# Holding both token halves of a linear open, and dividing the probabilities in place

## The chip, the cores and the metric

The kernel runs on one core of one Trainium2 chip. The metric is the device time of one execution in microseconds (us), lower is better. The kernel before took 2855.56 us, the median of 3 runs (2854.57 to 2858.59).

## What is computed

One inference step of a trunk of two layers with 1024 channels, for 128 context tokens and 512 latent tokens, 640 tokens in all. Cut to what matters here, a layer is:

```
h   = rms_norm(x) * (1 + scale1) + shift1
cb, cc, cx, aq, ak, av, dn_q, dn_k, dn_v, dn_z, dn_beta, dn_a, gate_logits = split(h @ w_in)
ya  = (cb * conv3(cc * cx)) @ w_pa                                  # short gated convolution
yb  = softmax(q @ keys.T * 128**-0.5) @ vals @ w_pb                 # 8 heads, 2 key-value heads
yc  = gated_deltanet_both_directions(dn_q, dn_k, dn_v, ...) @ w_pc  # 4 heads, chunked scan
mix = (ga * ya + gb * yb + gc * yc) @ w_o
x   = x + gate1 * rms_norm(mix)
ffn = (silu(h2 @ w_gate) * (h2 @ w_up)) @ w_down                    # h2: norm of x, 2816 wide
x   = x + gate2 * rms_norm(ffn)
```

Context tokens attend to themselves (128 keys); latent tokens attend to 128 cached keys and their own 512, so a row of probabilities has 640 entries. All data are fp32.

## The kernel before

Activations lie channel by token: a tile has 128 channels on the partitions and 640 tokens in the free dimension, and each is kept as a pair of fp32r tiles, a rounded high part and the rest (`hh`). A **linear** computes 128 output channels for all 640 tokens. Its weights come in blocks of up to four k-tiles (128x128 each). For a block, the SP queue starts a DMA into one of three raw tiles (`wraw`, tag `wr`, NWR = 3); ScalarE casts it to the high part `whi`, VectorE subtracts to get `wlo` (`split`, lines 93 to 95); `whi` and `wlo` have three buffers each (NW = 3). Each k-tile takes three matmuls (`mm3`, lines 362 to 365): high by high, high by low, low by high. The 640 tokens are done as two halves of 320 columns, each in a PSUM bank of its own from a ring of three (`lbank`, NL = 3). `linear` (lines 394 to 398) loads all blocks and runs `lin_half` for half 0 over all k-tiles, then for half 1. After a half, `ev` moves the sums out of the bank, on ScalarE or VectorE according to the linear: `sg` and `fs` (gates and feed-forward), `ccs`, `padc`, `padf`, `cz` (convolution and DeltaNet inputs). Most linears have eight k-tiles, in two blocks; `w_pa` and `w_pc` have four, in one; the first part of the down projection has 14, in four. `group` and the last six linears of `lin_res` keep their weight blocks and call `lin_half` themselves.

**Attention** (`attn_head`, lines 695 to 780). Per head there are three stages: query tiles 1 and 2, query tiles 3 and 4 (256 latent queries at a time), and the prompt. `a_sample` computes scores with queries on the partitions; `soft` (lines 702 to 724) takes the maximum, lets ScalarE write exp to `p` (128 queries by 640 keys) with its row sums, and inverts the sum on VectorE. It then builds `dg`, the identity times the inverse, from a ring of two tiles (NDG). `b_sample` multiplies `p` by `dg` on TensorE, key tile by key tile, into the tile `ptT` (lines 759 to 768): this transposes `p` and divides it by its sum in one step. The result is split and multiplied by the values (lines 775 to 777), into `po`. The prompt does the same at line 738 (`psp`) on 128 keys. The main loop (lines 1278 to 1293) keeps up to two stages (NPD = 2) between the softmax and the transposes.

**Order.** The program is written as generators: a main chain (DeltaNet, then attention) whose steps yield assumed costs, and a fill chain of linears that `run` and `weave` place between them. The tile framework then plans the order of the instructions on each engine before the run, by priority and its own model of when things are ready. On the chip each engine takes its queue in that order and waits by semaphores. The DeltaNet stretch of a layer has a long chain on VectorE (the elimination of lines 977 to 982, into `Tt`) and loads rows broadcast over partitions on the SP queue (`rowb`, line 899).

Of the kernel before, what the change touches and what calls it, by code (L numbers as in the profile page):

```python
# [14 lines left out]
P = 128  # L15
NT = 640
HF = NT // 2
# [13 lines left out]
NL, NB = 3, 5  # L31
NH_, NC_, NF_, NT_ = 16, 24, 16, 4
NWR, NW = 3, 3
NXO, NRR, NVW, NDG = 3, 3, 2, 2

KEEP = ("C", "C", "C", "C", "E", None)
LEAD = ("C", "C", "C", "C", "E")
# [15 lines left out]
def tile_trunk(ctx: ExitStack, tc: tile.TileContext, I: dict, O: list, layers=DEPTH):  # L53
    nc = tc.nc
    V, A, T, G, SY = nc.vector, nc.scalar, nc.tensor, nc.gpsimd, nc.sync
# [5 lines left out]
    def slot(name, shape=(P, NT), dt=F32, tag="F"):  # L61
        n = {"H": NH_, "C": NC_, "F": NF_}[tag]
        return sb.tile(list(shape), dt, tag=tag, name=name, bufs=n)

    def cslot(name, shape=(P, NT), dt=F32):
        return slot(name, shape, dt, "C")
# [4 lines left out]
    def lbank():  # L71
        return pp.tile([P, 512], F32, tag="l", name="l", bufs=NL)

    def bank(name):
        return pp.tile([P, 512], F32, tag="c", name=name, bufs=NB)

    def small(name, shape, bufs, dt=F32):
        return sb.tile(list(shape), dt, tag=name, name=name, bufs=bufs)

    def hv(t, h):  # L80
        return t[:, h * HF:(h + 1) * HF]
# [11 lines left out]
    def split(hi, lo, src):  # L93
        A.copy(hi, src)  # L94
        V.tensor_sub(lo, src, hi.bitcast(F32))  # L95
# [7 lines left out]
    ident = small("ident", (P, P), 1)  # L103
# [115 lines left out]
    pt = bank("c2")  # L219
# [137 lines left out]
    def wblock(src, nk, keep=None):  # L357
        raw = sb.tile([P, nk, P], F32, tag="wr", name="wraw", bufs=NWR)
        SY.dma_start(out=raw, in_=src.rearrange("(k p) f -> p k f", p=P))
        return wsplit(raw, [P, nk, P], keep)  # L360

    def mm3(out, wh, wl, ah, al, first, last):
        T.matmul(out, lhsT=wh, rhs=ah, start=first, stop=False)  # L363
        T.matmul(out, lhsT=wh, rhs=al, start=False, stop=False)  # L364
        T.matmul(out, lhsT=wl, rhs=ah, start=False, stop=last)  # L365

    def wblocks(src, nk, keep=None):
        out = []
        k = 0
        if keep == "E":  # L370
            hi, lo = [sb.tile([P, 8, P], F32R, tag="E", name="wk", bufs=3) for _ in range(2)]
            for k in range(0, nk, 4):
                raw = sb.tile([P, 4, P], F32, tag="wr", name="wraw", bufs=NWR)
                SY.dma_start(out=raw, in_=src[k * P:(k + 4) * P].rearrange("(k p) f -> p k f", p=P))
                split(hi[:, k:k + 4], lo[:, k:k + 4], raw)
            return [(hi, lo, nk)]
        while k < nk:
            n = min(4, nk - k)
            hi, lo = wblock(src[k * P:(k + n) * P], n, keep)
            out.append((hi, lo, n))  # L380
            k += n
        return out

    def lin_half(blocks, acts, h, ev):
        pb = lbank()[:, :HF]
        i = 0
        for hi, lo, nk in blocks:
            for j in range(nk):
                ah, al = acts[i]
                mm3(pb, hi[:, j, :], lo[:, j, :], hv(ah, h), hv(al, h), i == 0, i == len(acts) - 1)  # L390
                i += 1
        ev(h, pb)

    def linear(src, acts, ev):

        bl = wblocks(src, len(acts))
        for h in range(2):
            lin_half(bl, acts, h, ev)

    def group(items, side=None):  # L400

# [47 lines left out]
    def lin_res(srcw, acts, ys, gs, keeps, part, after, end=False):  # L449
# [20 lines left out]
        for m in range(n0):  # L470
            linear(w(m), acts, ev(m))
# [33 lines left out]
    def gate(l, b, m, tag="F"):  # L505

        c0 = COL["gate"] + b * D + m * P
        sg = slot("sg", tag=tag)
        linear(I["w_in"][l, :, c0:c0 + P], cur["h"], sig_ev(sg))
        return sg  # L510
# [184 lines left out]
    def attn_head(l, h, kv, qs):  # L695
        KT, KP, Vh, Vl = kv
        g = h // 4
        qh, ql, rq = qs[h]
        of = slot(f"o{h}")
        hd = slice(g * P, (g + 1) * P)  # L700

        def soft(c, parts):

            n = sum(x.shape[-1] for x in parts)
            nb, s = small("nb", (P, 2), 4), small("ssum", (P, 2), 4)
            rc = rq[:, 2 * c:2 * c + 1]
            for i, x in enumerate(parts):
                V.tensor_reduce(out=nb[:, i:i + 1], in_=x, axis=AX.X, op=ALU.max, negate=True)
            if len(parts) == 2:
                V.scalar_tensor_tensor(out=nb[:, 0:1], in0=nb[:, 0:1], scalar=nb[:, 1:2], in1=rc, op0=ALU.min, op1=ALU.mult)  # L710
            else:
                V.tensor_mul(nb[:, 0:1], nb[:, 0:1], rc)
            p = cslot("p", (P, n))
            o_ = 0
            for i, x in enumerate(parts):
                w = x.shape[-1]
                A.activation(p[:, o_:o_ + w], x, AF.Exp, scale=rc, bias=nb[:, 0:1], accum_out=s[:, i:i + 1])
                o_ += w
            if len(parts) == 2:
                V.tensor_add(s[:, 0:1], s[:, 0:1], s[:, 1:2])  # L720
            V.reciprocal(s[:, 0:1], s[:, 0:1])
            dg = small("dg", (P, P), NDG)
            V.tensor_scalar_mul(dg, ident, s[:, 0:1])
            return p, dg


        kh, kl = KT[g]
        kp = KP[g]

        def a_prompt():  # L730
            psc = bank("psc")[:, :P]
            mm3(psc, qh[:, 0:P], ql[:, 0:P], kp[:, 0, :], kp[:, 1, :], True, True)
            return [soft(0, [psc])]

        def b_prompt(sm_):
            p, dg = sm_[0]
            psc = bank("psp")
            T.matmul(psc[:, 0:P], lhsT=p, rhs=dg, start=True, stop=True)
            pth = cslot("pth", (P, 2, P), F32R)
            split(pth[:, 0, :], pth[:, 1, :], psc[:, 0:P])  # L740
            mm3(psc[:, P:2 * P], Vh[0][:, 0, hd], Vl[0][:, 0, hd], pth[:, 0, :], pth[:, 1, :], True, True)
            A.copy(of[:, 0:P], psc[:, P:2 * P])

        def a_sample(pr2):
            out = []
            for c in (1 + 2 * pr2, 2 + 2 * pr2):
                cs = slice(c * P, (c + 1) * P)
                parts = []
                for h_ in range(2):
                    b = bank("sco")[:, :HF]  # L750
                    mm3(b, qh[:, cs], ql[:, cs], hv(kh, h_), hv(kl, h_), True, True)
                    parts.append(b)
                out.append(soft(c, parts))
            return out

        def b_sample(pr2, sm_):
            tt = []
            for j in range(3):
                pt = bank("ptT").rearrange("p (i n) -> p i n", i=2)
                m = 2 if j < 2 else 1  # L760
                for i in range(m):
                    kt = 2 * j + i
                    for q in range(2):
                        T.matmul(pt[:, i, q * P:(q + 1) * P], lhsT=sm_[q][0][:, kt * P:(kt + 1) * P], rhs=sm_[q][1],  # L764
                                 start=True, stop=True)
                th, tl = cslot("pTh", (P, 2, 256), F32R), cslot("pTl", (P, 2, 256), F32R)
                split(th[:, :m], tl[:, :m], pt[:, :m])
                tt.append((th, tl))
            po = bank("po")[:, 0:256]
            for kt in range(5):  # L770
                vi = 5 if kt == 0 else kt
                vh, vl = Vh[vi // 2][:, vi % 2, hd], Vl[vi // 2][:, vi % 2, hd]
                th, tl = tt[kt // 2]
                th, tl = th[:, kt % 2, :], tl[:, kt % 2, :]
                T.matmul(po, lhsT=vh, rhs=th, start=(kt == 0), stop=False)  # L775
                T.matmul(po, lhsT=vl, rhs=th, start=False, stop=False)
                T.matmul(po, lhsT=vh, rhs=tl, start=False, stop=(kt == 4))  # L777
            A.copy(of[:, P + pr2 * 256:P + (pr2 + 1) * 256], po)

        return [(a_sample, b_sample, 0), (a_sample, b_sample, 1), (a_prompt, b_prompt, None)], of  # L780


# [466 lines left out]
    for p in range(2):  # L1249
        mod_first(p)  # L1250
        if p == 0:
            first = lead(0)
            for i in range(1, NLD):
                w, a, ev, k = first[3][i]
# [6 lines left out]
    for l in range(layers):  # L1261
# [61 lines left out]
        acts, acts2 = [], []  # L1323
# [77 lines left out]
```

## Time and profile before

| | us |
|---|---|
| median of 3 runs | 2855.56 |
| lowest, highest | 2854.57, 2858.59 |
| the profiled execution | 2858.44 |
| its span, first instruction to last | 2856.7 |

| engine | busy us | share of the span | instructions |
|---|---|---|---|
| PE (TensorE matmul) | 2767.4 | 97% | 20042 |
| PEld (its weight loads, beside PE) | 2637.4 | 92% | 20042 |
| DVE (VectorE) | 1539.8 | 54% | 3275 |
| ACT (ScalarE) | 1252.4 | 44% | 2863 |
| POOL (GpSimd) | 112.2 | 4% | 235 |

One execution is profiled, so durations are of that execution, and its own time is set beside them. PE's busy time is the union of records that overlap one another: a matmul's record spans its way through the array, and the next starts before it ends. The distance from start to start says what one costs in a stream. "Idle before, releaser" is the time an engine stood still before an instruction and what ended that. The granted clock (PEclk) is 1.00 at 2.4 GHz and 0.50 at 1.2 GHz; its mean is 0.984. The layers' stages lie, for layer 0 and layer 1, at about 80 to 560 and 1500 to 2000 us (DeltaNet, convolution and gates), 588 to 791 and 2013 to 2210 us (attention), and 950 to 1450 and 2360 to 2800 us (feed-forward).

### The profile page before, as it was taken

The page shows a single profiled execution, that of the slowest core. Times are in us where ns is not written, and L with a number is a line of the kernel's source. Part 1 is how long each engine was busy: PE and PEld are TensorE (multiplying, and loading weights), DVE is VectorE, ACT ScalarE, POOL GpSimd, SP SyncE. Part 2 cuts the span into 40 slices and gives each one's busy share as a digit, 9 for nine tenths or more (in the row PEclk, how much of TensorE's full clock was granted, in tenths as well). Part 3 has the DMA queues.
Part 4 walks back from the last instruction along what each step waited for, and adds up shares of the span by engine and source line. Part 5 has one row for each costly group of instructions (what it writes and reads, how often), then busy time and mean ns, then how long its engine had stood idle before and what let it go on. Part 6 is the DMA issues. An engine that isn't in the chain of part 4 may idle for free.

```text
span 2856.7 us, 50458 instructions
## 1 busy us (share of the span) xinstructions
PE 2767.4 (97%) x20042; PEld 2637.4 (92%) x20042; DVE 1539.8 (54%) x3275; ACT 1252.4 (44%) x2863; POOL 112.2 (4%) x235
## 2 busy tenths in 40 slices
PE   7999999999999999999989899999999999999998
PEld 4898998999999899999978889989999999999997
DVE  4576566466643744224465765764677446442344
ACT  4433543465534533223455335435655354332334
POOL 1000000000000200000020000000000020000002
PEclk9999999999999999999999999999999999999999
DMA  7441354333364444444443423443232433222232
GB/s 245 75 83 43 83 102 114 81 64 91 116 183 135 145 131 141 130 154 144 133 114 72 74 44 83 102 99 84 62 93 90 115 105 97 75 73 77 73 111 75
DMA packets 401562, 293.52 MB, mean 103 GB/s; under 512 B 19318, under 2 KB 365228, under 8 KB 401324
## 3 DMA queue, kind: packets, MB, share of 16 engines
q1 hardware_dynamic: 401324, 290.28, 38.9%
q8 instruction: 157, 2.57, 0.4%
q14 instruction: 81, 0.66, 0.1%
HBM read 257.10 MB, written 33.11 MB: 102 GB/s over the span
## 4 chain that ended last, share of the span: by engine, by line
PE 80%; DVE 8%; DMA 7%; ACT 3%; issue 2%; POOL 0%; SPq 0%; DVEq 0%; ACTq 0%; POOLq 0%
PE l L363 21%; PE l L365 21%; PE l L364 21%; DMA rowb<-gd 3%; PE ptT L764 3%; DMA wraw<-in_w_in_dram 2%; PE pm L324 1%; DVE wlo L95 1%; DVE Tt L982 1%; DVE tmpE L980 1%; PE sco L363 1%; PE po L775 1%; PE po L777 1%; PE scan L1061 1%; PE sco L365 1%
## 5 line engine op out<-in xcount | busy, mean ns | idle before, releaser
L95 DVE TENSOR_TENSOR wlo<-wraw,whi 128x512 fp32r<-128x512 f32 (+1 forms) x540 | 370.2, 687 | 587.9 <-ACT whi L94 575.2
L94 ACT CAST whi<-wraw 128x512 fp32r<-128x512 f32 (+1 forms) x540 | 330.4, 613 | 733.6 <-PE l L364 654.6
L363 PE MATMUL l<-hh,whi 128*128 128x320 f32 x1856 | 593.4, 320 | 16.1 <-ACT whi L94 14.2
L365 PE MATMUL l<-hh,wlo 128*128 128x320 f32 x1856 | 588.1, 317 | 10.9 <-DVE wlo L95 10.9
L364 PE MATMUL l<-hl,whi 128*128 128x320 f32 x1856 | 584.7, 315 | 0.0
L363 PE MATMUL l<-h2h,whi 128*128 128x320 f32 x1248 | 387.7, 311 | 0.0
L364 PE MATMUL l<-h2l,whi 128*128 128x320 f32 x1248 | 385.8, 309 | 0.0
L365 PE MATMUL l<-h2h,wlo 128*128 128x320 f32 x1248 | 385.7, 309 | 0.0
L363 PEld LDWEIGHTS l<-hh,whi 128*128 128x128 f32 x1856 | 355.2, 191 | 21.6 <-ACT whi L94 16.4
L365 PEld LDWEIGHTS l<-hh,wlo 128*128 128x128 f32 x1856 | 355.1, 191 | 16.3 <-DVE wlo L95 15.0
L364 PEld LDWEIGHTS l<-hl,whi 128*128 128x128 f32 x1856 | 355.0, 191 | 1.9
L363 PEld LDWEIGHTS l<-h2h,whi 128*128 128x128 f32 x1248 | 234.7, 188 | 7.0 <-ACT fs L417 3.1
L364 PEld LDWEIGHTS l<-h2l,whi 128*128 128x128 f32 x1248 | 234.7, 188 | 0.0
L365 PEld LDWEIGHTS l<-h2h,wlo 128*128 128x128 f32 x1248 | 234.7, 188 | 0.0
L363 PE MATMUL l<-ah,whi 128*128 128x320 f32 x544 | 170.3, 314 | 0.0
L365 PE MATMUL l<-ah,wlo 128*128 128x320 f32 x544 | 168.0, 309 | 0.0
L364 PE MATMUL l<-al,whi 128*128 128x320 f32 x544 | 167.9, 309 | 0.0
L152 POOL TENSOR_TENSOR acc<-acc,sqt 128x320 f32<-128x320 f32 x88 | 86.3, 980 | 2020.8 <-ACT sqt L148 2018.3
L364 PE MATMUL l<-rsl,whi 128*128 128x320 f32 x384 | 119.0, 311 | 0.2
L365 PE MATMUL l<-rsh,wlo 128*128 128x320 f32 x384 | 119.0, 310 | 0.0
L363 PE MATMUL l<-rsh,whi 128*128 128x320 f32 x384 | 118.3, 312 | 0.0
L363 PEld LDWEIGHTS l<-ah,whi 128*128 128x128 f32 x544 | 102.3, 188 | 5.0 <-ACT whi L94 2.8
(428 smaller groups left out, 5477.7 us busy)
## 6 DMA issues: line engine op xcount, KB each, us to landing
wraw<-in_w_in_dram SPq DMA_DIRECT2D x256, 256.0 KB, 4.6
wm<-in_w_mod_dram SPq DMA_DIRECT2D x80, 512.0 KB, 5.7
wraw<-in_w_gate_dram SPq DMA_DIRECT2D x88, 256.0 KB, 3.0
wraw<-in_w_up_dram SPq DMA_DIRECT2D x88, 256.0 KB, 3.1
wraw<-in_w_down_dram SPq DMA_DIRECT2D x80, 256.0 KB, 3.1
rowb<-gd SPq DMA_DIRECT2D x32, 320.0 KB, 9.4
mixo<-mixd SPq DMA_DIRECT2D x32, 320.0 KB, 6.6
wm<-in_w_mod_dram SPq DMA_DIRECT2D x32, 256.0 KB, 3.9
```

The source lines that it names most:

```text
L94: A.copy(hi, src)
L95: V.tensor_sub(lo, src, hi.bitcast(F32))
L152: (V if n == 2 else G).tensor_add(accs[0], accs[0], t)
L324: T.matmul(pm[32 * u:32 * u + 2, 0:256], lhsT=sc[:, k, :], rhs=w[:, u * 256:(u + 1) * 256], start=(n == 0), stop=(n == KD - 1))
L363: T.matmul(out, lhsT=wh, rhs=ah, start=first, stop=False)
L364: T.matmul(out, lhsT=wh, rhs=al, start=False, stop=False)
L365: T.matmul(out, lhsT=wl, rhs=ah, start=False, stop=last)
L764: T.matmul(pt[:, i, q * P:(q + 1) * P], lhsT=sm_[q][0][:, kt * P:(kt + 1) * P], rhs=sm_[q][1], start=True, stop=True)
L775: T.matmul(po, lhsT=vh, rhs=th, start=(kt == 0), stop=False)
L777: T.matmul(po, lhsT=vh, rhs=tl, start=False, stop=(kt == 4))
L980: V.tensor_tensor(out=tv, in0=Tt[:, j + 1:32, j:j + 1].to_broadcast([P, n, j]), in1=Tt[:, j:j + 1, 0:j].to_broadcast([P, n, j]), op=ALU.mult)
L982: V.tensor_add(Tt[:, j + 1:32, 0:j], Tt[:, j + 1:32, 0:j], tv)
```

## The change

`linear` opens a bank for each half at its first block. Each weight block is used for half 0 and then for half 1 before the next block; a half's `ev` follows its last block. The three matmuls of a k-tile and their order are the same. In `soft`, VectorE multiplies `p` by the inverse sum in place; `dg` and its ring are gone, and `ptT` and `psp` are filled by transposes of `p` with the identity.

```diff
 def linear(src, acts, ev):
-    bl = wblocks(src, len(acts))
-    for h in range(2):
-        lin_half(bl, acts, h, ev)
+    pb = {}
+    i0 = 0
+    for hi, lo, nk in wblocks(src, len(acts)):
+        for h in range(2):
+            if i0 == 0:
+                pb[h] = lbank()[:, :HF]
+            for j in range(nk):
+                ah, al = acts[i0 + j]
+                mm3(pb[h], hi[:, j, :], lo[:, j, :], hv(ah, h), hv(al, h), i0 + j == 0, i0 + j == len(acts) - 1)
+            if i0 + nk == len(acts):
+                ev(h, pb[h])
+        i0 += nk
...
             V.reciprocal(s[:, 0:1], s[:, 0:1])
-            dg = small("dg", (P, P), NDG)
-            V.tensor_scalar_mul(dg, ident, s[:, 0:1])
-            return p, dg
+            V.tensor_scalar_mul(p, p, s[:, 0:1])
+            return p
...
-            T.matmul(psc[:, 0:P], lhsT=p, rhs=dg, start=True, stop=True)
+            T.transpose(psc[:, 0:P], sm_[0], ident)
...
-                        T.matmul(pt[:, i, q * P:(q + 1) * P], lhsT=sm_[q][0][:, kt * P:(kt + 1) * P], rhs=sm_[q][1],
-                                 start=True, stop=True)
+                        T.transpose(pt[:, i, q * P:(q + 1) * P], sm_[q][:, kt * P:(kt + 1) * P], ident)
```

## Rows read from the trace of the kernel before

**Rows 1.** The page: busy time (share, instructions), then the chain that ended last.
```profile
PE 2767.4 (97%) x20042; PEld 2637.4 (92%) x20042; DVE 1539.8 (54%) x3275; ACT 1252.4 (44%) x2863; POOL 112.2 (4%) x235
...
PE 80%; DVE 8%; DMA 7%; ACT 3%; issue 2%; POOL 0%; SPq 0%; DVEq 0%; ACTq 0%; POOLq 0%
PE l L363 21%; PE l L365 21%; PE l L364 21%; DMA rowb<-gd 3%; PE ptT L764 3%; DMA wraw<-in_w_in_dram 2%; PE pm L324 1%; DVE wlo L95 1%; DVE Tt L982 1%; DVE tmpE L980 1%; PE sco L363 1%; PE po L775 1%; PE po L777 1%; PE scan L1061 1%; PE sco L365 1%
```

**Rows 2.** Groups by line and form on PE: count, busy us, mean ns, idle before.
```profile
L764 PE MATMUL ptT<-dg,p 128*128 128x128 f32 x640 | 84.5, 280 | 0.0
...
L893 PE MATMUL nat<-ident,dz 128*128 128x128 f32 x80 | 11.7, 277 | 3.8 <-DVE dz L869 3.8
...
L738 PE MATMUL psp<-dg,p 128*128 128x128 f32 x32 | 6.2, 276 | 0.2 <-ACT p L717 0.2
```

**Rows 3.** Timeline of PE in three places: start us, duration, instruction.
```profile
602.13 2.39 PE L764 MATMUL ptT<-dg,p 128*128 128x128 f32 x20
604.27 0.39 PE L365 MATMUL l<-hh,wlo 128*128 128x320 f32 x1
...
1156.07 0.31 PE L364 MATMUL l<-h2l,whi 128*128 128x320 f32 x1
...
1156.51 0.31 PE L364 MATMUL l<-h2l,whi 128*128 128x320 f32 x1
...
1812.87 1.25 PE L893 MATMUL nat<-ident,dz 128*128 128x128 f32 x10
1813.96 1.28 PE L938 MATMUL kk<-dz 128*128 128x128 f32 x10
```

**Rows 4.** What PE waited for: us in total, times, longest.
```profile
PE l L363 <- ACT whi L94: 14.2, 6, 6.3
PE l L365 <- DVE wlo L95: 10.9, 13, 2.3
...
PE l L363 <- ACT sg L417: 1.9, 2, 1.0
```

**Rows 5.** Timeline of 434 to 440 us, one linear that begins at 435.85.
```profile
434.14 0.62 ACT L94 CAST whi<-wraw 128x512 fp32r<-128x512 f32 x1 [1.25 <-PE l L364]
...
435.85 0.31 PE L363 MATMUL l<-hh,whi 128*128 128x320 f32 x1
435.90 0.62 ACT L94 CAST whi<-wraw 128x512 fp32r<-128x512 f32 x1 [1.14 <-PE l L364]
...
437.61 0.31 PE L363 MATMUL l<-hh,whi 128*128 128x320 f32 x1
...
437.75 0.31 PE L364 MATMUL l<-hl,whi 128*128 128x320 f32 x1
...
439.10 0.69 DVE L95 TENSOR_TENSOR wlo<-wraw,whi 128x512 fp32r<-128x512 f32 x1
...
439.85 0.41 PE L365 MATMUL l<-hh,wlo 128*128 128x320 f32 x1 [1.79 <-DVE wlo L95]
```

**Rows 6.** Timeline of PE: the first and the last such wait.
```profile
123.29 0.41 PE L363 MATMUL l<-hh,whi 128*128 128x320 f32 x1 [2.98 <-ACT whi L94]
...
1866.20 0.41 PE L365 MATMUL l<-hh,wlo 128*128 128x320 f32 x1 [1.79 <-DVE wlo L95]
```

**Rows 7.** Short stretches: length, busy us (instructions), granted clock, DMA share, GB/s.
```profile
125.20:128.60 3.40, 3.40 (x15) 3.40 (x14) 1.64 (x2) 1.62 (x4) 0.00 (x0) 0.50 0.73 177
...
1593.00:1596.40 3.40, 3.40 (x14) 3.40 (x14) 3.29 (x8) 0.00 (x0) 0.00 (x0) 0.50 0.31 75
1610.00:1616.90 6.90, 3.20 (x11) 2.98 (x12) 3.18 (x7) 1.86 (x3) 0.00 (x0) 0.51 0.60 107
1812.80:1816.20 3.40, 3.40 (x30) 3.19 (x28) 1.31 (x3) 3.28 (x8) 0.00 (x0) 1.00 0.25 40
```

**Rows 8.** The two attention stretches: length, busy of PE, PEld, DVE, ACT, POOL.
```profile
588.00:791.00 203.00, 202.24 (x1519) 197.08 (x1518) 140.23 (x389) 118.58 (x323) 0.00 (x0) 1.00 0.33 96
2013.00:2210.00 197.00, 196.69 (x1467) 193.41 (x1466) 135.50 (x384) 114.57 (x316) 0.00 (x0) 1.00 0.29 80
```

**Rows 9.** VectorE lines 723 and 556: ns min/median/max; idle before line 723.
```profile
L723 DVE TENSOR_SCALAR dg<-ident,ssum x80: 267/286/291, 591.3 to 2207.6; 128x128 f32<-128x128 f32 x80
...
  PE ptT L764: 4.1, 10
  PE psp L738: 3.5, 10
...
L556 DVE TENSOR_SCALAR cy<-padf,cols x8: 547/550/557, 138.7 to 1659.3; 128x641 f32<-128x641 f32 x8
```

More of the change, by code (lines that the diff above doesn't have):

```diff
@@ L33 @@
 NWR, NW = 3, 3
-NXO, NRR, NVW, NDG = 3, 3, 2, 2
+NXO, NRR, NVW = 3, 3, 2
 KEEP = ("C", "C", "C", "C", "E", None)
@@ L735, in b_prompt @@
         def b_prompt(sm_):
-            p, dg = sm_[0]
             psc = bank("psp")
-            T.matmul(psc[:, 0:P], lhsT=p, rhs=dg, start=True, stop=True)
+            T.transpose(psc[:, 0:P], sm_[0], ident)
             pth = cslot("pth", (P, 2, P), F32R)
```

## The prediction

> **What bounds the kernel now.** I read the page first. TensorE is busy 97% of a 2856.7 us span, VectorE 54%, ScalarE 44%; in the chain that ended last TensorE holds 80%, and lines 363 to 365, the three matmuls of a linear, hold 21% each [rows 1]. So an instruction taken from TensorE shortens the run as long as nothing else comes due late, and one added to another engine costs only where TensorE waits for it.
>
> Second, the instruction groups, to see which PE instructions the change touches [rows 2]. The reader should compare counts with the program. The matmul by the diagonal is called 320 times at line 764 (16 heads of both layers x 2 query pairs x 5 key tiles x 2 queries), yet the row counts 640: this fp32 matmul is issued as two instructions. Line 738 likewise: 16 calls, 32 instructions. `nat` at line 893 is a true transpose of 128x128 fp32, called 80 times, and its row counts 80: one instruction each.
>
> Third, the timeline, for the spacing of starts, since a matmul's own duration (0.31 us) overlaps its neighbours. In a linear a start follows every 0.147 us (1156.07 to 1156.51 for three), so a linear of eight k-tiles (2 halves x 8 x 3 = 48 matmuls) takes 7.04 us, twelve matmuls 1.76 us. Twenty instructions of line 764 take 2.14 us (602.13 to 604.27); ten `nat` transposes take 1.09 us (1812.87 to 1813.96) [rows 3].
>
> Fourth, what PE waits for. Two rows stand out: 14.2 us for a cast weight block (6 times) and 10.9 us for its low part (13 times) [rows 4]. I counted where they fall. In the example, the linear begins at 435.85, the twelve matmuls of its first block go by, and at the second block, at the 15th matmul, PE stands still for 1.79 us until the split of 439.10 is done [rows 5]. Eleven linears have such a wait of more than 0.5 us, the first at 123.29 and the last at 1866.20 [rows 6], and in all eleven it is the 13th or the 15th matmul: the second block, first half. All lie in the DeltaNet stretches.
>
> Fifth, stretches: behind six of these waits the granted clock is 0.50 (the lower level, 1.2 GHz), five times for 3.4 us and once for 6.9 us; the first and the last of the five and the long one are shown [rows 7].
>
> **The change, part by part.** (1) *Transposes.* Per query pair twenty instructions become ten: 2.14 - 1.09 = 1.05 us, 32 times, 33.6 us. The prompt's 16 drop one of two instructions of 2.14 / 20 = 0.107 us: 1.7 us. Together 35.3 us, inside stretches where PE is busy 202.2 of 203 and 196.7 of 197 us [rows 8], so I count all of it. From the other side: zero if the transposes too came out as pairs; at most half of the busy row of line 764, 42 us [rows 2].
>
> What the row shows of the clock: at 1812.80 to 1816.20, with ten transposes in it, the granted clock is 1.00 [rows 7]. The Trainium skill, "TensorE: Matmul & The Clock Gate", Part 4 (PE-mode transpose), says that transposes do not count as activity of TensorE as matmuls do, so that the full clock does not engage in them. By that rule the change could lower the clock in attention; the trace agrees with it nowhere so far, and it is a rival below.
>
> (2) *Division in place.* `dg` (128x128) took 0.286 us on VectorE; `p` has 640 columns, and the nearest row is the scalar multiply of 128x641 at line 556, 0.550 us [rows 9]. 64 tiles x 0.264 = 17 us more VectorE work (the 16 prompt tiles stay 128 wide). VectorE is busy 140 of 203 us there [rows 8]; with 8.5 us more in a stretch 18 us shorter that is 149 of 185, 80%. What hides it is the pipeline of two stages between softmax and transposes. If that cover went, at most the 17 us show. On the other side the ring of two `dg` tiles goes, on which VectorE stood 4.1 + 3.5 us behind the transposes [rows 9]. Behind the longer multiply on VectorE's queue stand the weight splits, and PE waits for those. I take 2 us, nearer to the low end, as PE hardly waits in these stretches.
>
> (3) *Order in a linear.* No matmul is added or removed. Before, a block's buffer is read last at matmuls 36 and 48, so the casts that wait for one come in pairs: 434.14 and 435.90, both released by PE [rows 5]. With the new order the first block ends at matmul 24 and the second block is first needed at matmul 25 instead of 13: 1.76 us later, or, for the other blocks, the buffer comes free 1.76 us sooner. Each of the eleven waits should shrink by 1.76 us. Eight are longer and give 8 x 1.76 = 14.1 us, three are shorter and give their 0.9, 0.7 and 1.0: 16.7 us, of the 25.1 in [rows 4]. What then comes late is the transfer itself: the 6.3 us wait keeps 4.5. Shorter waits take four of the five 3.4 us dips with them (half speed, so 1.7 us each): 6.8 us; bounds are 0 and all six, 11.9 us. The first dip and the long one stay, with waits of over 1 us left.
>
> What it adds: both halves of a linear hold a bank until its end, and there are three banks. The next linear's second half needs the bank of this one's first half; that eviction had 7.0 us and now has 1.76 + 1.76 = 3.5 us. The trace shows a slack of 3.5 us already, at the one-block linears (24 matmuls; 16 per layer, untouched): two waits of 1.9 us in all for an eviction by ScalarE [rows 4], 0.06 us for each of 32. With 117 linears per layer of two or more blocks, 234 x 0.06 = 14 us is the upper estimate and zero the lower (if the earlier casts leave ScalarE freer, no less). I take 4, nearer to the low end: 49 of the 117 lie in the feed-forward part, where PE waits for no eviction of a plain linear.
>
> The rest (`group`, the kept blocks of `lin_res`, the score and value products) is not touched; DMAs are the same in number. In the down projection (14 k-tiles, four blocks, three buffers) the halves are interleaved before too, since the fourth block needs the first one's buffer.
>
> **Sum.** -35.3 + 2 - 16.7 - 6.8 + 4 = -52.8 us. The profiled execution took 2858.4 us (span and 1.7 us around it), so 2805.6; the median of the runs shown is 2.9 us lower, so I predict 2802.7.
>
> **Rivals.** (a) Only the transposes pay: where the cast waits for a transfer, a later need moves the wait and does not end it, and the planner, which orders every engine anew, puts other work ahead of the split. For it: several waits sit behind DMA landings in the DeltaNet stretch. Against: the wait of [rows 5] had its data and only needed time. 2858.4 - 35.3 + 6 - 2.9 = 2826.
>
> (b) VectorE becomes the bound in attention and all 17 us of its added work shows on PE: 2802.7 + 15 = 2818. For it: 80% busy, one queue in order. Against: splits have more slack than before.
>
> (c) The other side: the bank. If an eviction misses its 3.5 us at every second linear of several blocks by the 0.95 us of the two waits seen, 117 x 0.95 = 111 us, and the time is 2914. It decides above 52.8 / 234 = 0.23 us per linear. For it: ScalarE and VectorE take their queues in order, and both stand for microseconds on late transfers in the DeltaNet stretches. Against: two such waits at 32 linears that have this slack now.
>
> (d) The clock falls behind the runs of transposes. One dip of 3.4 us for each of the 32 costs 1.7 x 32 = 54 us, which eats the whole gain: 2857. With dips of 6.9 us, 110 us: 2913. Against it: [rows 7], 1.00 with ten transposes, and in attention linears stand between the runs. This is what the rule of the skill named above would do here.
>
> (e) The change does not do what it says: `transpose` of `p` comes out as two instructions, so (1) is lost: 2838. Against: 80 for 80 at `nat`.
>
> **Chances.** Forecast 0.60, (a) 0.20, (b) 0.08, (c) 0.05, (d) 0.04, (e) 0.03. The forecast's own range is 2783 to 2813: below, all waits and dips of [rows 4, 7] vanish (25.1 + 11.9 instead of 23.5, no price paid: 2783); above, the bank price is 14 us instead of 4. The stated range goes up to 2834 to take in (a), (b) and their share of bank waits, and down to 2780. A difference under 0.2% (5.7 us) can't be told from none. Faster: forecast, (a), (b), (e), 0.91; same 0.03, from (d); slower 0.06, from (c) and (d).
>
> **What would show it.** Right: line 764 or its successor at 320 instructions with some 1.1 us per run of ten, each attention stretch 18 us shorter with PE still over 98% busy; waits of PE for the cast and the low part at some 8 us instead of 25.1, at the 25th matmul; fewer stretches at clock 0.50. Wrong: PE waiting for `sg`, `fs`, `padc` or `ccs` evictions (c); for low parts inside attention (b); clock 0.50 in attention (d); 640 instructions (e). The prediction falls if PE's idle time in the DeltaNet stretches stays above 25 us, or if a wait for a bank totals more than 14.

## The result and the profile after

The changed kernel takes 2824.07 us, the median of 4 runs (2820.49 to 2829.99), against 2855.14 us for the kernel before beside it (4 runs). The ratio is 0.9891, 95% interval 0.9871 to 0.991: 31 us faster. The sign was right, but the forecast was 2802.7: of the 52.8 us expected, 31 came. The time lies inside the stated range (2780 to 2834), yet above the forecast's own (2783 to 2813), in the part that was added for the rivals. The profiled execution of the changed kernel took 2820.49 us (span 2818.6), 3.6 us under its median, and the one of before lay 3.3 us above its own; so from profile to profile the gain is 38 us, and the accounts below are of that pair.

The page of the changed kernel: busy time, and the chain that ended last, by engine and by line (they answer to [rows 1]).

```profile
PE 2724.1 (97%) x19706; PEld 2594.3 (92%) x19706; DVE 1554.2 (55%) x3275; ACT 1250.4 (44%) x2863; POOL 114.2 (4%) x235
...
PE 78%; DVE 8%; DMA 8%; ACT 3%; issue 2%; SPq 0%; POOL 0%; DVEq 0%; ACTq 0%; POOLq 0%
PE l L363 21%; PE l L364 21%; PE l L365 21%; DMA rowb<-gd 3%; DMA wraw<-in_w_in_dram 2%; PE pm L324 1%; DVE wlo L95 1%; PE ptT L772 1%; PE po L782 1%; DVE tmpE L987 1%; DVE Tt L989 1%; PE sco L363 1%; DMA wm<-in_w_mod_dram 1%; PE scan L1068 1%; PE po L784 1%
```

PE has 336 instructions fewer, which is 320 + 16, and the transposes' share of the chain is 1% where the products with `dg` had 3%. VectorE has 14.4 us more work. The transposes by line (duration minimum, median, maximum in ns), answering to [rows 2]:

```profile
L772 PE MATMUL ptT<-ident,p x320: 270/273/329, 603.8 to 2169.0; 128*128 128x128 f32 x160
...
L746 PE MATMUL psp<-ident,p x16: 270/271/329, 625.6 to 2169.7; 128*128 128x128 f32 x16
```

320 and 16: one instruction for each call. The timeline of PE in attention (start us, duration, instruction), answering to [rows 3]:

```profile
658.17 0.60 PE L772 MATMUL ptT<-ident,p 128*128 128x128 f32 x4
658.52 0.39 PE L363 MATMUL l<-hh,whi 128*128 128x320 f32 x1
658.75 0.60 PE L772 MATMUL ptT<-ident,p 128*128 128x128 f32 x4
659.11 0.40 PE L364 MATMUL l<-hl,whi 128*128 128x320 f32 x1
...
772.01 1.03 PE L772 MATMUL ptT<-ident,p 128*128 128x128 f32 x8
```

Eight in a row start 0.109 us apart ((1.03 - 0.27) / 7), as the `nat` transposes did. Matmuls of linears cut the transposes of the 32 query pairs into 73 runs; the products with `dg` came in 61. The first matmul behind a run starts early, some 0.03 us after the last transpose, and the next start then follows after 0.23 us (658.52 to 658.75). Taken together nothing is lost: four transposes and one matmul of a linear take 0.58 us (658.17 to 658.75), which is 4 x 0.109 + 0.147.

What PE waited for on lines 363 and 365 (us in total, times, longest), answering to [rows 4]:

```profile
PE l L363 <- ACT padc L864: 10.5, 5, 3.0
...
PE l L363 <- DVE sg L442: 4.7, 4, 1.5
...
PE l L363 <- DVE Tt L989: 3.5, 2, 1.8
...
PE l L363 <- ACT ccs L447: 1.4, 2, 1.1
...
PE l L363 <- ACT sg L427: 1.4, 3, 0.5
...
PE l L365 <- DVE wlo L95: 1.0, 1, 1.0
```

The two large rows of before, the cast and the low part, are gone but for 1.0 us. In their place stand the lines that move a half's sums out of its bank (`padc`, `sg`, `ccs`) and VectorE's elimination (`Tt`), between whose steps evictions are queued. Over all rows of these two lines, waits for weights went from 26.3 to 3.2 us and waits for evictions from 4.2 to 25.2: an exchange, to within some 2 us.

The two attention stretches, cut at the first score and the last prompt transpose (length, busy of PE, PEld, DVE, ACT, POOL, granted clock, DMA share, GB/s), first of the changed kernel, then with the same cuts of the one before; they answer to [rows 8].

```profile
588.70:775.60 186.90, 183.37 (x1359) 174.16 (x1358) 144.39 (x386) 115.16 (x318) 0.00 (x0) 1.00 0.39 109
1989.60:2171.80 182.20, 178.94 (x1295) 172.70 (x1294) 143.51 (x384) 114.30 (x316) 0.00 (x0) 1.00 0.28 86
```

```profile
587.20:786.20 199.00, 198.37 (x1495) 193.54 (x1494) 135.70 (x383) 114.91 (x316) 0.00 (x0) 1.00 0.32 92
2013.50:2209.90 196.40, 196.09 (x1463) 192.81 (x1462) 135.25 (x382) 114.47 (x316) 0.00 (x0) 1.00 0.29 80
```

They are 12.1 and 14.2 us shorter, 18 each were expected. The clock stayed at 1.00. PE, which stood still for 0.6 and 0.3 us, now stands for 3.5 and 3.3. The first stretch holds 136 PE instructions fewer and not 168, so 32 other ones moved into it, at 0.147 us some 4.7 us of work that is saved elsewhere.

From the two traces I made one account: the span, PE's idle time between its first and its last instruction, that on lines 363 and 365 for weights and for evictions, the time in stretches of granted clock 0.50, and the rest (span less idle less half of the low clock's time), all in us.

| kernel | span | PE idle | for weights | for evictions | clock 0.50 | rest |
|---|---|---|---|---|---|---|
| before | 2856.7 | 79.6 | 26.3 | 4.2 | 89.5 | 2732.3 |
| after | 2818.6 | 84.6 | 3.2 | 25.2 | 70.5 | 2698.7 |

The gain of 38.1 is 33.6 of PE work (what is left over when the others are taken out) and 9.5 of clock (half of 19.0), less 5.0 of new idle time.

### The profile page after: what moved, and what is told of

It reads as the page before. It is cut to its first block, busy times and chain, and to the rows that moved or that the text cites. A ratio compares the mean times of both kernels' runs of the same rounds, so it can differ in the third digit from the quotient of the medians.

```text
span 2818.6 us, 49773 instructions
## 1 busy us (share of the span) xinstructions
PE 2724.1 (97%) x19706; PEld 2594.3 (92%) x19706; DVE 1554.2 (55%) x3275; ACT 1250.4 (44%) x2863; POOL 114.2 (4%) x235
## 2 busy tenths in 40 slices
DMA packets 401557, 293.45 MB, mean 104 GB/s; under 512 B 19318, under 2 KB 365228, under 8 KB 401324
## 3 DMA queue, kind: packets, MB, share of 16 engines
q1 hardware_dynamic: 401324, 290.28, 40.1%
## 4 chain that ended last, share of the span: by engine, by line
PE 78%; DVE 8%; DMA 8%; ACT 3%; issue 2%; SPq 0%; POOL 0%; DVEq 0%; ACTq 0%; POOLq 0%
PE l L363 21%; PE l L364 21%; PE l L365 21%; DMA rowb<-gd 3%; DMA wraw<-in_w_in_dram 2%; PE pm L324 1%; DVE wlo L95 1%; PE ptT L772 1%; PE po L782 1%; DVE tmpE L987 1%; DVE Tt L989 1%; PE sco L363 1%; DMA wm<-in_w_mod_dram 1%; PE scan L1068 1%; PE po L784 1%
```

## The experiments

Theory 1 was that the new order of the linears only exchanges waits for weight blocks for waits for banks. Theory 1a, made after the first set of runs, was that both kinds of wait have one cause: in the DeltaNet stretches ScalarE or VectorE stands at a late row load, and whatever is queued behind it, splits or evictions, comes late. The rivals: that the transposes fell short by themselves, that VectorE's longer division shows, or that banks (or weight buffers) alone set the loss. Each ratio is to the kernel before, run on the same chip beside it; differences between kernels of different sets are taken from ratios, times 2856 us.

**One part at a time.** The first keeps the old order of `linear` and has the transposes and the division:

```diff
 def linear(src, acts, ev):        # as before
     bl = wblocks(src, len(acts))
     for h in range(2):
         lin_half(bl, acts, h, ev)
...
+            V.tensor_scalar_mul(p, p, s[:, 0:1])
...
+            T.transpose(psc[:, 0:P], sm_[0], ident)
```

> The kernel before with the transposes and the division in place alone; the order of the linears is the old one. Theory 1 (the order of the linears only exchanges waits for weight blocks for waits for banks): this part carries nearly all of the gain, 28 to 36 us, so 2820 to 2827 us, with PE's waits for the cast and low parts still at about 25 us. Theory 2 (attention runs into VectorE or ScalarE, the linears carry the gain): 10 to 18 us, so 2837 to 2845 us, with PE idle in attention.

Measured: 2837.06 us (2831.88 to 2839.44), 0.993 (0.9916 to 0.9943), 20 us less. That gain lies between the two expectations and confirms neither. Its attention stretches are 186.7 and 182.3 us, as in the changed kernel, and its waits for weights are nearly those of before:

```profile
PE l L365 <- DVE wlo L95: 11.3, 16, 2.2
PE l L363 <- ACT whi L94: 9.8, 7, 4.3
```

The second is the new order alone, with `dg` as before:

```diff
 def linear(src, acts, ev):        # as in the change
...
             dg = small("dg", (P, P), NDG)
             V.tensor_scalar_mul(dg, ident, s[:, 0:1])
             return p, dg
```

> The kernel before with the new order of the linears alone; probabilities are still divided by the matmul with the diagonal. Theory 1: within 8 us of before, 2847 to 2858 us; PE's waits for the cast and low parts fall from 25 us to under 4, and waits for evictions (padc, sg, ccs, and whatever runs ahead of them) rise from about 4 to about 20. Theory 2: 16 to 24 us faster, 2831 to 2839 us.

Measured: 2850.32 us (2846.12 to 2851.2), 0.9973 (0.9963 to 0.9983), 7.7 us less, as theory 1 expected. The exchange is all there without a transpose: waits for weights 2.3 us, for evictions 25.5. Its rows:

```profile
PE l L363 <- ACT padc L867: 9.3, 4, 3.5
...
PE l L363 <- DVE sg L442: 5.1, 4, 1.6
...
PE l L363 <- DVE cz L594: 3.4, 1, 3.4
PE l L363 <- DVE Tt L992: 3.3, 2, 1.7
```

The third divides in place in the old order, but multiplies by the identity instead of transposing:

```diff
-            dg = small("dg", (P, P), NDG)
-            V.tensor_scalar_mul(dg, ident, s[:, 0:1])
-            return p, dg
+            V.tensor_scalar_mul(p, p, s[:, 0:1])
+            return p
...
-                        T.matmul(pt[:, i, q * P:(q + 1) * P], lhsT=sm_[q][0][:, kt * P:(kt + 1) * P], rhs=sm_[q][1],
-                                 start=True, stop=True)
+                        T.matmul(pt[:, i, q * P:(q + 1) * P], lhsT=sm_[q][:, kt * P:(kt + 1) * P], rhs=ident, start=True, stop=True)
```

> The kernel before with the probabilities divided in place, but turned by plain matmuls with the identity (two instructions each, as before). It has the added VectorE work of 17 us and none of the saved TensorE work. If that work is hidden by the two stages between softmax and transposes: within 4 us of before, 2851 to 2859 us, perhaps 2 us faster as the ring of two diagonals is gone. If VectorE's work shows: 8 to 17 us slower, 2863 to 2872.

Measured: 2857.39 us (2851.98 to 2861.5), 0.9997 (0.9988 to 1.0006); attention 199.1 and 196.0 us. VectorE's added work costs nothing that can be measured.

**A fourth bank.** Linears get four banks and the rest of the program four instead of five, first in the changed kernel, then, as the control, with the old order and the transposes.

```diff
-NL, NB = 3, 5
+NL, NB = 4, 4
```

> The changed kernel with four banks for the linears and four instead of five for everything else. Theory 1 (evictions have too little slack with three banks): PE's waits of lines 363 to 365 for evictions fall from about 22 us to under 8, worth 10 to 18 us in the linears; four banks for the rest may cost something in attention, where two softmax tiles alone take four, so 2806 to 2825 us. Rival (the evictions are late because PE outruns ScalarE and VectorE for good, so one more bank only delays the wait): waits stay above 15 us, time 2822 to 2835.

> The transposes with the old order of the linears, and four banks for the linears, four for the rest: the control for the changed kernel with four and four (2846.7 us). If the bank is what takes back the gain of the new order, then with four banks the new order must show its worth: this one waits for weights as with three banks (20 us or more) and is 15 to 25 us slower than 2846.7, 2862 to 2872 us. If the same late ScalarE and VectorE work catches the linear whatever it waits for, the two lie within 8 us: 2839 to 2855.

Measured: 2846.69 us (2840.6 to 2852.7), 0.9962 (0.9948 to 0.9976) for the first, by the ratios 20 us slower than the change and outside both expectations; and 2862.27 (2856.17 to 2869.14), 1.0019 (1.0009 to 1.0029) for the control, within the first of its two. The waits for evictions did go, to under 3 us, but taking a bank from the rest costs about 25 us by itself (0.993 to 1.0019), and waits for the split came back. The first kernel's rows:

```profile
PE pn L157 <- DVE acc L152: 23.4, 7, 4.2
PE l L365 <- DVE wlo L95: 10.1, 11, 2.7
...
PE ptT L772 <- ACT p L727: 4.8, 6, 2.6
```

So a fourth bank shows that the eviction waits are bank waits, but its time can't price them. With four banks the new order was worth 16 us (1.0019 to 0.9962), with three 11 (0.993 to 0.9891): not the whole of the 21 us that the evictions cost.

**No row loads.** What keeps the evictions? In the changed kernel, ScalarE between 120 and 129 us (start us, duration, instruction, idle before and its releaser), and under it PE:

```profile
121.34 0.61 ACT L94 CAST whi<-wraw 128x512 fp32r<-128x512 f32 x1
127.53 0.21 ACT L959 ACTIVATE egl<-rowb 128x5 f32<-128x5 f32 x1 [5.59 <-DMA rowb<-gd]
127.65 0.47 ACT L864 COPY padc<-l 128x128 f32<-128x128 f32 x2
128.01 0.63 ACT L94 CAST whi<-wraw 128x512 fp32r<-128x512 f32 x1
...
124.90 0.31 PE L365 MATMUL l<-hh,wlo 128*128 128x320 f32 x1
128.17 0.42 PE L363 MATMUL l<-hh,whi 128*128 128x320 f32 x1 [2.96 <-ACT padc L864]
```

ScalarE stands 5.59 us at a small exponential that needs a broadcast row, and the copy that empties the bank is next in its queue; 0.5 us after that copy begins, PE goes on. In the kernel before, the same instruction at the same place was followed by a cast, and PE waited for that; the wait is the first row of [rows 6]:

```profile
122.52 0.21 ACT L952 ACTIVATE egl<-rowb 128x5 f32<-128x5 f32 x1 [5.77 <-DMA rowb<-gd]
122.63 1.12 ACT L94 CAST whi<-wraw 128x512 fp32r<-128x512 f32 x2
```

The next two kernels put constants in place of the 32 row loads, in the changed kernel and in the one with the transposes alone.

```diff
     def rowb(l, s, dh):
-        t = small("rowb", (P, 5, P), 2)
-        SY.dma_start(out=t, in_=gd[l][s, :, dh, :].partition_broadcast(P))
-        return t
+        if s not in rowc:
+            t = rowc[s] = small("rowb", (P, 5, P), 2)
+            V.memset(t, 0.5 if s else -3000.0)
+        return rowc[s]
```

> The changed kernel without the 32 broadcast row loads (rowb): two constant tiles stand for them, so the decays are wrong and their DMAs are gone. Theory 1a (a late row load holds ScalarE and VectorE, and evictions queue behind it): PE's waits for padc vanish (10.5 us before), all waits for evictions fall from 25 to under 14, and the time falls by 12 to 25 us against the changed kernel, 2799 to 2812 us. Rival (the elimination and the steady load of the two engines make them): waits for evictions stay above 18, time within 10 us, 2814 to 2826.

> The same without row loads, with the transposes and the old order of the linears. Theory 1a: the waits for weight blocks have the same cause, and fall from 22 to under 10 us; against the transposes alone (2837) 12 to 30 us less, 2807 to 2825, and the two orders come within 6 us of each other. Rival: weight waits stay above 16, 2827 to 2840.

Measured: 2783.45 us (2781.37 to 2785.31), 0.974 (0.9726 to 0.9754), and 2791.05 (2784.61 to 2792.02), 0.9764 (0.9752 to 0.9777). Both gained more than was expected. Waits for evictions went from 25.2 to 3.0 us in the one, waits for weights from 21.8 to 0.3 in the other, and the two orders stand 7 us apart instead of 11 (within 6 was expected). So both kinds of wait, as a whole, come of the row loads.

How a row load gets to PE is seen for about half of it. I followed each wait of over 0.5 us in the DeltaNet stretches back through the queues. Of 20.9 us for evictions in the changed kernel, 8.0 stand right behind ScalarE's wait for a row load, 2.9 behind work on rows that VectorE had waited for, 6.4 behind VectorE's elimination, which runs without a wait there, and 3.6 behind other work of ScalarE. Of 24.4 us for weights in the kernel before, 11.6 stand right behind a row load, 4.7 behind the elimination (the example of [rows 5] is one) and 8.1 behind a late transfer of weights; the cast that the longest wait ended with is this:

```profile
1613.03 0.62 ACT L94 CAST whi<-wraw 128x512 fp32r<-128x512 f32 x1 [9.09 <-DMA wraw<-in_w_in_dram]
```

A transfer in that stretch took 15.3 us to land, where the median of a `w_in` block is 4.6, and the blocks there are started on the same SP queue as the row loads, some 0.6 us behind two of them. So there is a rival path that theory 1a does not have, argued here and not tested: a row load holds up not an engine but the transfers behind it.

**A fourth weight buffer.** If the old order's waits are only late splits, one more buffer of `whi` and `wlo` should end them. It was paid for with smaller rings elsewhere:

```diff
-NH_, NC_, NF_, NT_ = 16, 24, 16, 4
-NWR, NW = 3, 3
-NXO, NRR, NVW = 3, 3, 2
+NH_, NC_, NF_, NT_ = 16, 24, 16, 3
+NWR, NW = 3, 4
+NXO, NRR, NVW = 2, 2, 2
```

> The transposes with the old order, and a fourth buffer for whi and wlo (room for it from one buffer less in three small rings). The weights get more slack without a second open bank. If the waits for weights come of too few buffers: they fall from 22 to under 12 us, evictions stay under 8, 2822 to 2831 us. If they come of transfers or of a split that is planned late: they stay above 17 us, 2833 to 2842.

Measured: 2837.65 us (2836.81 to 2847.24), 0.994 (0.9927 to 0.9953), no faster than with three. The waits for weights did fall, from 21.8 to 4.4 us, but others rose:

```profile
PE pn L157 <- DVE acc L152: 29.6, 7, 6.2
PE nat L890 <- DVE dz L866: 11.4, 6, 5.2
```

`pn` was 18.9 and `nat` 6.4 us with three buffers. Whether the smaller rings or the same row loads did that, this run doesn't tell; it is inconclusive on the time.

**Row loads that land sooner.** The rows lie in device memory as 2 x 5 x 8 x 128, so a load takes five runs of 128 numbers for every partition. Stored as 2 x 8 x 5 x 128, it takes one run of 640. Nothing is left out of these kernels; VectorE makes one small copy more per layer.

```diff
-    gd = [dr.tile([2, 5, 8, P], F32, name=f"gd{l}") for l in range(DEPTH)]
+    gd = [dr.tile([2, 8, 5, P], F32, name=f"gd{l}") for l in range(DEPTH)]
...
-        T.transpose(pr[0:80, P:2 * P], gb.rearrange("p a b c -> p (a b c)"), ident)
+        gbn = small("gbn", (P, 2, 8, 5), 1)
+        V.tensor_copy(gbn, gb.rearrange("p a b c -> p a c b"))
+        T.transpose(pr[0:80, P:2 * P], gbn.rearrange("p a c b -> p (a c b)"), ident)
...
-        SY.dma_start(out=t, in_=gd[l][s, :, dh, :].partition_broadcast(P))
+        SY.dma_start(out=t.rearrange("p c n -> p (c n)"), in_=gd[l][s, dh].rearrange("c d -> (c d)").partition_broadcast(P))
```

It was done in the changed kernel and in the one with the transposes alone, and then in the two without transposes (there with the copy in a scratch tile), the new order alone and the kernel before.

> The changed kernel with the decay and beta rows stored head by head, so that a broadcast load reads one run of 640 elements per partition instead of five of 128 (one small VectorE copy per layer added, nothing left out). Theory 1a (late row loads are the common cause of both kinds of wait): a load lands in under 6.5 us instead of 9.4, waits for evictions fall from 25 to under 12 us, 2793 to 2812 us. Rival (what helped without rows was the removed work and traffic as a whole): waits above 18, 2816 to 2828.

> The same row layout with the transposes and the old order of the linears. Theory 1a: weight waits fall from 22 to under 11 us, 2800 to 2820 us, and what the new order is worth shrinks from 13 us (2837 against 2824) to under 8. If the new order has a worth of its own that does not depend on late loads, it stays at 10 to 16 us.

> The new order of the linears and the new row layout, with the old division by the diagonal matmul (the small reordering copy uses another scratch tile). Against the changed kernel with row runs (2789.0) it prices the transposes without late row loads. If the late loads took part of their gain (20 of some 34 us): it grows to 28 to 36 us, 2817 to 2825. If attention's own drain and the start take it: it stays at 17 to 24 us, 2806 to 2813.

> The kernel before with the new row layout alone. If the two waits have one cause, the rows alone take 30 us or more off, and the order of the linears is worth under 6 us beside them: 0 to 6 us above l_row_runs, 2806 to 2828. If the order is worth something on its own: 8 us or more above l_row_runs.

| kernel with row runs | median us (lowest to highest) | ratio to before (95%) | without row runs | PE idle | for weights | for evictions | clock 0.50 | rest |
|---|---|---|---|---|---|---|---|---|
| both parts | 2788.98 (2785.91 to 2789.83) | 0.9761 (0.9747 to 0.9774) | 0.9891 | 61.7 | 0.6 | 3.7 | 67.1 | 2692.5 |
| transposes alone | 2794.22 (2783.68 to 2798.72) | 0.9771 (0.9753 to 0.979) | 0.993 | 66.1 | 1.2 | 3.7 | 79.5 | 2691.1 |
| new order alone | 2815.04 (2812.67 to 2816.58) | 0.9849 (0.9836 to 0.9863) | 0.9973 | 53.3 | 1.8 | 2.6 | 72.6 | 2724.4 |
| neither | 2814.24 (2813.07 to 2815.18) | 0.9849 (0.9835 to 0.9862) | 1 | 56.2 | 3.8 | 1.9 | 48.5 | 2733.0 |

The row loads of the changed kernel (KB each, median us from issue to landing), what ScalarE waited for them in all, and the tile's landing times (minimum, median, maximum):

```profile
rowb<-gd SPq DMA_DIRECT2D x32, 320.0 KB, 9.4
...
ACT egl L959 <- DMA rowb<-gd: 57.2, 14, 5.6
...
DMA to landing us min/median/max: 7.1/9.4/11.2
```

The same lines of the changed kernel with row runs:

```profile
rowb<-gd SPq DMA_DIRECT2D x32, 320.0 KB, 4.0
...
ACT egl L961 <- DMA rowb<-gd: 11.0, 13, 2.4
...
DMA to landing us min/median/max: 3.8/4.0/5.2
```

Both kernels with transposes came out faster than theory 1a expected (2793 to 2812, 2800 to 2820). With the new order alone the transposes are worth 25 us, between the two expectations; the kernel before with row runs met the expectation of one cause, and lies level with the new order. These runs don't tell the two paths apart. The bytes moved are the same (290.28 MB), and a `w_in` block lands in a median of 4.5 us in the kernel before with row runs, 4.6 without; but ScalarE's waits for such blocks fell too, from 46.3 to 33.8 us.

With the rows there sooner, each kind of wait is under 4 us in all four kernels, and the order of blocks in a linear is worth 2.9 us (0.9771 to 0.9761, the intervals overlap) or nothing (0.9849 and 0.9849). Beside the kernel before, the rows alone give 43 us, more than the change. Both parts with row runs is the fastest kernel with all of the computation in it: 68 us under the one before, 37 under the change, by the ratios.

What the transposes give can now be read four times, from ratios: 20 us (1 to 0.993), 23 (0.9973 to 0.9891), 22 (0.9849 to 0.9771) and 25 (0.9849 to 0.9761). The last is the least disturbed.

## Why the prediction was right in sign and too large

Its terms beside what the pair of profiles shows, in us:

| term | predicted | measured |
|---|---|---|
| (1) transposes, PE work (measured: what is left over) | -35.3 | -33.6 |
| (2) VectorE's longer division | +2 | 0 |
| idle in attention, not in the sum | none | +5.9 |
| (3) waits for weights | -16.7 | -23.1 |
| (3) clock | -6.8 | -9.5 |
| (3) the bank | +4 | +21.0 |
| other idle time | none | +1.2 |
| sum | -52.8 | -38.1 |

**The step that failed is the bank's price in (3): "I take 4, nearer to the low end".** It measured 21.0, outside its own upper bound of 14. The bound scaled 0.06 us from the one-block linears, and those gave waits only on `sg` [rows 4]; it did not hold for the other evictions of the DeltaNet stretches, where `padc`, `ccs` and `Tt` now give 15.4 of the 25.2 us, and ScalarE and VectorE stand at row loads. The two waits that the bound was scaled from came of row loads already. ScalarE before the first of them, and PE at it:

```profile
402.97 0.21 ACT L952 ACTIVATE egl<-rowb 128x5 f32<-128x5 f32 x1 [4.43 <-DMA rowb<-gd]
...
405.66 0.43 ACT L417 ACTIVATE sg<-l 128x320 f32<-128x320 f32 x1
...
406.14 0.41 PE L363 MATMUL l<-hh,whi 128*128 128x320 f32 x1 [1.04 <-ACT sg L417]
```

The second, at 1832.68, has a wait of 4.25 us for a row load at the same place. An average over 32 linears was taken of something that comes where a row load is late. I had written that both engines stand "for microseconds on late transfers" there as a point for rival (c), and did not put it into the bound. Rival (c)'s mechanism was there, at 21 / 234 = 0.09 us per linear, under its turning point of 0.23, so the sign held. Both conditions named for the prediction's fall came true: waits for a bank above 14 us, and PE idle in the two DeltaNet stretches at 17.4 + 14.5 = 31.9 us, above 25 (before: 17.0 + 18.7).

**Waits for weights** fell by more than the 1.76 us each. The long cast wait, of which 4.5 us were to stay, is gone too, in this kernel and with the new order alone; why that transfer is not late there was not followed. Two linears beyond the eleven had waited for over 0.5 us, at their third matmul (0.59 us at 418.03, 0.54 at 1844.37); those waits are gone as well. So (3) predicted the waits that go, and not that their cause stays. The slack moved: the old order gave an eviction 7.0 us and the split little, the new one gives the split more and an eviction 3.5. With row loads of 9.4 us one of the two is late in either order. That the row loads are the cause of the waits as a whole is shown by taking the loads away and by making them land in 4.0 us; that a particular wait of 2.96 us is due to one particular load is read from its timeline alone. Each kernel's order is planned anew, so some of what the smaller edits moved is the plan's.

**(1)** was right in its size on PE. From the first start of a run of `ptT` or `psp` to the second start behind it, with PE's waits and 0.147 us for the one matmul in between taken out, the runs took 77.8 us before (77 runs) and 41.7 after (89): 36.1 less. The 33.6 of the account are 2.5 lower; where those lie was not found. "I count all of it" was the weak half. The transposes end sooner than the work beside them can feed: PE stands at the products with the values, for `pTh` and `o`, at late scores and at late `wm` loads, +5.9 us. With the longer start (5.7 us, below) that leaves 24.5 of the 36.1, near the 20 to 25 us that the runs give for the transposes. The rows of the idle time for the second stretch:

```profile
PE po L782 <- ACT pTh L94: 1.2, 1, 1.2
PE psc L363 <- ACT p L727: 1.0, 1, 1.0
PE ptT L772 <- ACT o L750: 0.2, 1, 0.2
```

**(2)** was right: 0.9997 with the division alone; rival (b) is dead. Rival (e) too: 320 instructions. Rival (a) had the transposes pay alone and came out near the measured time (2826), but for another reason: the weights' waits did go, and others took their place.

**The clock.** Granted clock 1.00 stands in both attention rows above, with 336 transposes in them; rival (d) is dead. The Trainium skill, "TensorE: Matmul & The Clock Gate", Part 4 (PE-mode transpose), says that transposes do not count as activity of TensorE as matmuls do. Here, with runs of up to ten among matmuls, the trace shows no fall of the clock from it; a stretch of transposes alone was not run. Over the whole span the time at 0.50 fell by 19.0 us, with 14 falls of the clock instead of 17. But (3) was right there for less than the 9.5 us. The six falls behind waits for weights [rows 7] are gone, 23.9 us at 0.50; four new ones of 3.4 us stand behind the new waits, at 362.0, 1535.6, 1579.9 and 1764.7, the last of them here:

```profile
1765.00:1768.40 3.40, 3.40 (x15) 3.40 (x14) 2.94 (x4) 0.47 (x2) 0.00 (x0) 0.51 0.79 218
```

That is a gain of 5.1 us, where 6.8 were expected. The other 4.4 come from places at which no such wait changed, and no run shows that the change gives them: the mean clock of an execution goes from 0.984 to 0.987 in the four of the changed kernel, and from 0.983 to 0.989 in eighteen of the one before.

**Open.** The start, up to the gates of layer 0, takes 79.4 us in the profile before and 85.1 after; in the nine profiles with transposes it takes 82.8 to 89.0, in the five without 79.4 to 82.9, though no attention lies in it, and PE's instructions come in the same order there in the transposes alone and in the division alone. The rows from 57 to 80 us, of after and then of before:

```profile
57.00:80.00 23.00, 18.18 (x136) 13.32 (x136) 13.44 (x27) 11.18 (x28) 0.00 (x0) 0.98 0.95 168
```

```profile
57.00:80.00 23.00, 20.60 (x156) 15.68 (x157) 13.68 (x31) 12.48 (x36) 0.00 (x0) 1.00 0.82 167
```

The DMA engines are fuller (0.95 against 0.82) at the same GB/s, and PE gets 2.4 us less done. The cause was not found. Of the 5.7 us some 3 are idle time of PE and some 3 the clock (12.7 us at 0.50 up to there, 6.8 before); the table has them inside its other idle time and its clock. Open too: with the row loads gone, or landing sooner, the rest of the changed kernel's account is 6 to 8 us shorter (2698.7 to 2690.9 and 2692.5), beyond the waits and the clock.

## What to carry to other kernels

When an edit takes a wait away, follow the wait past the engine that released it, to what that engine was standing at: if that stays, the next thing in its queue is late instead. Two buffers that are freed by the same in-order engines (weights and banks here) share one slack, and reordering only moves it from one to the other. Before giving a stall more slack, see whether the transfer behind it can land sooner; here a change of layout gave 43 us where the reordering gave 8. A bound must be taken from the stretch at risk, not from like instructions in a quieter one.

## What the runs showed of the hardware

- A broadcast of 320 KB to 128 partitions landed in a median of 9.4 us as five runs of 512 bytes for each partition and in 4.0 us as one run of 2560. The queue's packets fell from 401324 to 384940, which is 32 loads x 128 partitions x 4. The Trainium skill, "Perfetto Trace Analysis", section DMA Optimizations, says that transfers under 2 KB carry a large overhead each and that joining them helps; the trace agrees, by a factor of 2.3 for this load.
- Four banks for linears and four for the rest, instead of three and five, cost about 25 us (0.993 to 1.0019), with the old order, which had 5.3 us of waits for evictions to lose.
- A 128x128 fp32 matmul against `dg` or the identity came as two instructions (640 for 320 calls) that start a median of 0.112 us apart, a transpose of the same tile as one (320 for 320), 0.109 us apart. Passing from a run of either to the matmuls of a linear cost nothing: from the last start of the run to the second start behind it, a median of 0.26 us in both kernels, which is one of these and 0.147.
